# Two-layer retention and block-attention trunk on one core: weights loaded by halves of 0.5 MB with fewer bytes queued, embedding inputs loaded later, one normalisation moved to ScalarE, more buffers for turned tiles

## The chip, the cores and the metric

The kernel runs on one NeuronCore of a Trainium2 chip. The metric is the device time of one execution in microseconds (us). The kernel before was timed in three runs; their median is 311.43 us.

## What is computed

Two decoder layers over x of 256 tokens by 1024, all in float32:

```
for i in range(2):
    h = rms_norm(x, norm_g[i])
    rq, rk, rv, rz, mq, mk, mv, mz = split(h @ w_in[i], 8)        # 1024 x 4096, 512 columns each
    r = groupnorm(retention(rotary(rq), rotary(rk), rv)) * ret_norm_g[i] * silu(rz)     # 4 heads of 128
    m = moba(rms_norm(mq), rms_norm(mk), mv, rel_bias) * silu(mz)                       # 4 heads of 128
    x = x + concat(r, m) @ w_out[i]                               # 1024 x 1024
    gate = sigmoid(rms_norm(x) @ w_ple_gate[i])                   # 1024 x 1024
    x = x + gate * rms_norm(p[i] @ w_ple[i], ple_norm_g[i])       # p[i]: 256 x 256
```

With 256 tokens there is one block, so the block attention is causal softmax attention with a bias by distance. Retention is linear attention with a fixed decay; its per-head normalisation subtracts the mean of 128 outputs and divides by their deviation.

## The kernel before

**Products.** A float32 operand is split into a high part (rounded to the short form that TensorE multiplies) and the remainder. One product of 128 tokens, 128 inner elements and 512 columns is then three matmuls, `mm3` (L314 high times high, L315 high times low weights, L316 low times high weights). There are 408 such triples, 200 in layer 0 and 208 in layer 1, counted with the embedding's (L580 to L582); a set of weights serves both token halves m.

**Weights.** `Stage` (L245) stands for a 512 x 512 piece of a weight matrix, 1 MB. `gen` waits for one of four buffers `wst` of 1 MB and has SP issue the load (L261). `cast` then makes, for each half (two rows of 128), the high part on ScalarE (ACT, L271, tile wh) and the low part on VectorE (DVE, L273, tile wl); there are six pairs of wh and wl. A half serves 12 matmuls of 512 columns.

**Turned tiles.** Activations must be transposed before they are multiplied. ACT separates the 16-bit halves of a tile (`halves`, L450, tile u), SP issues a transposing DMA (`turned`, L460, tile w), and DVE copies the result into place (L469): into T for the heads of queries and keys, into PS for the probabilities, into tmp for the next product's operand, whose high part ACT makes (L486) and whose low part DVE makes (L488).

**The order** of all engines but TensorE's rows is chosen while the program is written, by a planner (`Flow`, L80). It keeps a clock per engine and a model of the DMA queue (`dma`), and lays each chain's next step when its engine, its buffers and its predecessors are free by its own clocks; among the ready steps the one with the lowest key goes first. Weight loads are held back while the modelled queue is more than `BACKLOG` ahead (L115). On the chip the resulting instruction streams are fixed: an engine, and SP's queue of DMA issues too, runs in that order and waits at an instruction whose semaphore isn't there yet.

**A layer** (`layer`, L606) runs: the projections MQ, MK, RQ, RK, MZ, MV, RV, RZ; between their matmuls, at points that the planner picks (`tick`), the attention scores (L751), attention output (L762), retention scores (L813) and retention output (L762 again); then the output projection, the embedding product (`embed`, L550) and the gate product, whose results update x (`gated`, L938). In layer 1 the MQ and MK projections are interleaved. `load_p` (L590) loads the embedding's inputs: pf (256 KB) and its gain gb, spread to all partitions (512 KB).

`ret_norm` (L819) takes statistics of the retention output on DVE, the inverse root on GpSimd (POOL, L502), and writes the normalised output on DVE (L838) into a tile T; `ret_gate` multiplies it by the gate (L855).

## Time and profile before

| | us |
|---|---|
| runs of the kernel | 310.88, 313.27, 311.43 (median 311.43) |
| the profiled execution | 310.27 |
| its span, first to last instruction | 308.5 |

The profiled execution is one run recorded by the hardware profiler; 1.8 us of it lie outside the span. All places in time below are us from the span's start. Matmul ends are modelled, so the pace of TensorE (PE) is read from the starts of successive matmuls: 0.227 us for 512 columns. A weight load (PEld) belongs to the matmul behind it.

### The profile page before, as it was taken

To read this page: it belongs to the slowest core of one execution; us is meant where nothing else is said; L and a number is where in the kernel's file an instruction comes from. 1 tells how busy PE (TensorE), PEld (TensorE's weight loads), DVE (VectorE), ACT (ScalarE), POOL (GpSimd) and SP (SyncE) were. 2 spreads that over 40 slices of the span, in tenths; PEclk is the share of its full clock that TensorE was granted. 3 is DMA by queue.
4 is the path that set the end of the run, shared out by engine and by line. 5 is a ranking of instruction groups with operands and counts; after the bars stand their busy time and mean duration, and the time that the engine had idled before them with its cause. 6 is when DMAs were issued, how large, how long until landed. Compare 5 with 4: busy or idle time off the path is not lost.

```text
span 308.5 us, 4105 instructions
## 1 busy us (share of the span) xinstructions
PE 300.1 (97%) x1393; PEld 247.6 (80%) x1393; DVE 254.4 (82%) x470; ACT 204.3 (66%) x342; POOL 32.8 (11%) x43
## 2 busy tenths in 40 slices
PE   8999999999999999999999999899999999999993
PEld 3888888878888888887878888688888888888783
DVE  3896898889887785799999595999988689739972
ACT  5879965995552566887588695499545438479611
POOL 5032100000002200031002220000000220001300
PEclk9999999999999999999999999999999999999999
DMA  7999999899963487583977889788897435784011
GB/s 257 413 425 407 270 321 287 230 295 305 324 184 139 147 227 259 90 300 136 295 212 188 293 269 227 191 215 235 282 363 203 166 136 132 259 155 69 1 70 69
DMA packets 54853, 69.76 MB, mean 226 GB/s; under 512 B 45484, under 2 KB 46256, under 8 KB 48688
## 3 DMA queue, kind: packets, MB, share of 16 engines
q1 hardware_dynamic: 54824, 69.50, 74.8%
q8 instruction: 11, 0.18, 0.3%
q14 instruction: 10, 0.08, 0.1%
q10 hardware_dynamic: 8, 0.00, 0.0%
HBM read 57.42 MB, written 1.05 MB: 190 GB/s over the span
## 4 chain that ended last, share of the span: by engine, by line
PE 69%; DVE 15%; DMA 11%; issue 2%; POOL 1%; ACT 1%; POOLq 0%; ACTq 0%; DVEq 0%
PE acc L315 21%; PE acc L316 21%; PE acc L314 21%; DMA w<-u 10%; DVE wl L273 5%; PE mix L762 3%; DVE tmp L469 2%; DVE E L569 1%; DVE a L488 1%; PE mix L813 1%; DMA a<-in_first 1%; DVE x_t L902 1%; DVE T L469 1%; PE mix L751 1%; DVE tok L668 1%
## 5 line engine op out<-in xcount | busy, mean ns | idle before, releaser
L315 PE MATMUL acc<-wl,a 128*128 128x512 f32 (+1 forms) x392 | 151.7, 387 | 0.7 <-DVE wl L273 0.5
L314 PE MATMUL acc<-wh,a 128*128 128x512 f32 (+1 forms) x392 | 152.2, 388 | 0.0
L316 PE MATMUL acc<-wh,a 128*128 128x512 f32 (+1 forms) x392 | 151.0, 385 | 0.3 <-DVE her L565 0.3
L273 DVE TENSOR_TENSOR wl<-wst,wh 128x1024 fp32r<-128x1024 f32 x96 | 114.8, 1219 | 8.5 <-ACT wh L271 8.4
L271 ACT CAST wh<-wst 128x1024 fp32r<-128x1024 f32 x96 | 98.6, 1052 | 25.3 <-PE acc L316 21.8
L315 PEld LDWEIGHTS acc<-wl,a 128*128 128x128 f32 x392 | 73.7, 188 | 17.7 <-DVE wl L273 2.1
L314 PEld LDWEIGHTS acc<-wh,a 128*128 128x128 f32 x392 | 73.8, 188 | 15.1 <-ACT wh L363 0.4
L316 PEld LDWEIGHTS acc<-wh,a 128*128 128x128 f32 x392 | 73.7, 188 | 15.2 <-DVE a L488 0.7
L450 ACT COPY u<-tok 128x1024 uint16<-128x1024 uint16 x30 | 31.5, 1049 | 19.7 <-DVE tok L668 7.4
L469 DVE COPY tmp<-w 128x512 uint16<-128x512 uint16 x40 | 16.5, 457 | 10.5 <-DMA w<-u 10.5
L486 ACT CAST a<-tmp 128x512 fp32r<-128x512 f32 x20 | 12.4, 622 | 18.3 <-DVE tmp L469 9.5
L502 POOL TENSOR_TENSOR ro<-rs_t,neghalf 128x4 f32<-128x4 f32 x4 | 7.7, 1914 | 132.7 <-DVE rs_t L500 132.7
L469 DVE COPY T<-w 128x512 uint16<-128x512 uint16 x32 | 12.8, 457 | 7.0 <-DMA w<-u 6.7
L450 ACT COPY u<-x_t 128x1024 uint16<-128x1024 uint16 x12 | 12.5, 1045 | 5.8 <-DVE x_t L902 3.4
L943 ACT ACTIVATE tmp<-acc,hr 128x512 f32<-128x512 f32 (+1 forms) x9 | 5.8, 640 | 12.8 <-PE acc L316 9.2
L488 DVE TENSOR_TENSOR a<-tmp,a 128x512 fp32r<-128x512 f32 x20 | 13.7, 684 | 0.0
L502 POOL TENSOR_TENSOR er<-rs_t,neghalf 128x1 f32<-128x1 f32 x4 | 4.9, 1230 | 67.3 <-DVE rs_t L500 63.2
L762 PEld LDWEIGHTS mix<-V,PS 128*128 128x128 f32 x96 | 11.3, 192 | 0.3
L644 POOL TENSOR_TENSOR qr<-qms,neghalf 128x4 f32<-128x4 f32 x8 | 8.4, 1063 | 28.7 <-DVE qms L642 15.9
L762 PE MATMUL mix<-V,PS 128*128 128x128 f32 x96 | 11.4, 275 | 0.0
L733 ACT ACTIVATE tok<-tok,nm 128x128 f32<-128x128 f32 (+1 forms) x16 | 7.1, 447 | 5.4 <-DVE nm L730 5.4
L946 DVE SCALAR_TENSOR_TENSOR tmp<-tmp,E 128x512 f32<-128x512 f32 (+1 forms) x9 | 5.6, 627 | 4.4 <-ACT tmp L943 4.4
(86 smaller groups left out, 241.1 us busy)
## 6 DMA issues: line engine op xcount, KB each, us to landing
wst<-in_w_in SPq DMA_DIRECT2D x30, 1024.0 KB, 5.6
wst<-in_w_out SPq DMA_DIRECT2D x8, 1024.0 KB, 5.8
wst<-in_w_gate SPq DMA_DIRECT2D x8, 1024.0 KB, 5.2
wst<-in_w_ple SPq DMA_DIRECT2D x2, 1024.0 KB, 5.0
wst<-in_rest SPq DMA_DIRECT2D x4, 384.0 KB, 7.0
a<-in_rest SPq DMA_DIRECT2D x3, 384.0 KB, 4.9
x_t<-in_x SPq DMA_DIRECT2D x2, 512.0 KB, 10.1
gb<-in_ple_g SPq DMA_DIRECT2D x2, 512.0 KB, 5.4
```

What stands on the lines that cost most here:

```text
L271: nc.scalar.copy(hi, s)
L273: nc.vector.tensor_tensor(lo, s, hi.bitcast(F32), op=ALU.subtract)
L314: nc.tensor.matmul(ps, ah, wh[:, kk, cols], start=start, stop=False)
L315: nc.tensor.matmul(ps, ah, wl[:, kk, cols], start=False, stop=False)
L316: nc.tensor.matmul(ps, al, wh[:, kk, cols], start=False, stop=stop)
L450: nc.scalar.copy(u, src.bitcast(U16).rearrange("p (n t) -> p t n", t=2))
L469: nc.vector.tensor_copy(v, w[:, t].rearrange("p (h b) k -> p h (b k)", h=v.shape[1]))
L486: nc.scalar.copy(h, src)
L488: nc.vector.tensor_tensor(a.lo[:, k0:k0 + 4, m * P:(m + 1) * P], src, h.bitcast(F32), op=ALU.subtract)
L502: nc.gpsimd.tensor_tensor(dst, t[:, :n], neghalf[:, :n], op=ALU.pow)
L644: nc.gpsimd.tensor_tensor(r, t, neghalf[:, :H], op=ALU.pow)
L762: nc.tensor.matmul(ps[:, h * DH:(h + 1) * DH], lhs(h, m, b), v[:, b, h * DH:(h + 1) * DH], start=b == 0, stop=b == m)
```

## The change

Weights are loaded by halves: 96 loads of 0.5 MB into eight buffers, instead of 48 of 1 MB into four (the same bytes in the same space). The planner's allowance for queued bytes is 9.0 us of its queue model early in the program, then 1.5, then 0.7 (before: none early, then 3.0). The embedding's inputs are loaded at the MV projection instead of right after MK. x is loaded in one DMA. The normalised retention output is written by ACT as scale times input plus bias, for which DVE makes a small tile mr. There are four u and three w buffers instead of three and two; the small statistics tiles have four buffers per name instead of eight. Keys (a higher number is less urgent) of two chains move: the embedding's normalisation from -5 to -2, the squares from 3 to 8. In the last layer the two outputs of the first 512 columns leave in one DMA. The matmuls are the same in number and kind; the planner sets the attention scores of each layer two triples earlier among them.

```diff
-BACKLOG = 3.0
-U_BUFS, W_BUFS, T_BUFS = 3, 2, 3
+U_BUFS, W_BUFS, T_BUFS = 4, 3, 3
...
-        return r if mb is None or self.dma < 30 else max(r, self.dma - BACKLOG)
+        return r if mb is None else max(r, self.dma - self.backlog())
+
+    def backlog(self):
+        return 9.0 if self.dma < 30 else 1.5 if self.dma < 60 else 0.7
...
-    wst_p = pool("wst", 4)
+    wst_p = pool("wst", 8)
...
-    sm = pool("sm", 8)
+    sm = pool("sm", 4)
...
-                flow.begin(self.gen(), lambda: due(2 * self.i) - 10, 0.0)
-
-        def gen(self):
-            yield ask(SP, 0.45, take=("wst",), mb=1.0)
-            self.st = wst_p.tile([P, 4, GW], F32, name="wst")
-            nc.sync.dma_start(self.st, self.src)
-            yield ask(SP, 0.0)
-            for c in range(2):
-                self.chains[c] = flow.begin(self.cast(c), lambda c=c: due(2 * self.i + c) - 7, flow.end)
-
-        def cast(self, c):
+                for c in range(2):
+                    self.chains[c] = flow.begin(self.gen(c), lambda c=c: due(2 * self.i + c) - 7, 0.0)
+
+        def gen(self, c):
+            yield ask(SP, 0.42, take=("wst",), mb=0.5)
+            s = wst_p.tile([P, 2, GW], F32, name="wst")
+            nc.sync.dma_start(s, self.src[:, 2 * c:2 * c + 2])
             yield ask(ACT, 0.955, take=("w",))
...
-    L_X = [flow.begin(load(lambda m=m: x_t[:, m], lambda m=m: x[:, m], 0.5), 10.0 + m, 0.0) for m in range(MT)]
+    L_X = flow.begin(load(lambda: x_t, lambda: x, 1.0), 10.0, 0.0)
...
-            ST_X[l, m, "E"] = flow.begin(scaled(m, ps), flow.soon(-5))
+            ST_X[l, m, "E"] = flow.begin(scaled(m, ps), flow.soon(-2))
...
+            mr = small(H, "mr")
+            yield ask(DVE, 0.15)
+            nc.vector.scalar_tensor_tensor(mr, mv[:, :, 0], -1.0, r2, op0=ALU.mult, op1=ALU.mult)
             for h in range(H):
                 sl = slice(h * DH, (h + 1) * DH)
-                yield ask(DVE, 0.32, take=() if m or h else ("T",))
+                yield ask(ACT, 0.19, take=() if m or h else ("T",))
...
-                nc.vector.tensor_scalar(o[:, sl], ps[:, sl], mv[:, h, 0:1], r2[:, h:h + 1],
-                                        op0=ALU.subtract, op1=ALU.mult)
+                nc.scalar.activation(o[:, sl], ps[:, sl], AF.Identity, bias=mr[:, h:h + 1], scale=r2[:, h:h + 1])
...
-        load_p(l)
         for g in ORDER[2:]:
+            if g == MV:
+                load_p(l)
             project((g,), by_m=g == RZ)
...
-            sq.append(flow.begin(squares([xs], SQ[m][:, n:n + 1]), flow.soon(3), flow.end))
+            sq.append(flow.begin(squares([xs], SQ[m][:, n:n + 1]), flow.soon(8), flow.end))
```

**SP's queue, layer 1, around the turned queries and keys of the attention.** w<-u is a turned tile; the last of the four before the scores is the second half of MK. Before:

```order
L241 DMA pf<-in_pT 128x512
L241 DMA gb<-in_ple_g 128x1024
L261 DMA wst<-in_w_in 128x2048
L460 DMA_TRANSPOSE w_1886<-u_1874 128x8x128
L261 DMA wst<-in_w_in 128x2048
L460 DMA_TRANSPOSE w_1914<-u_1900 128x8x128
```

After:

```order
L265 DMA wst<-in_w_in 128x1024
L455 DMA_TRANSPOSE w_1950<-u_1937 128x8x128
L265 DMA wst<-in_w_in 128x1024
L455 DMA_TRANSPOSE w_1982<-u_1958 128x8x128
L265 DMA wst<-in_w_in 128x1024 x4
```

One half of 0.5 MB stands ahead of each turned tile instead of a whole 1 MB (128x2048), and the loads of pf and gb are gone from here.

**DVE, layer 0, from the attention's third row of scores to the first low weights of MV.** L730 (after: L725) is the maximum of the scores, L663, L665 and L668 the rotary step of RK, L469 (after: L464) the copies of turned probabilities into PS. The last row of each piece begins with the low weights of MV's first half. Before:

```order
L730 TENSOR_REDUCE nm<-tok 128x2
L663 TENSOR_TENSOR tmp<-acc,cst 128x512
L665 TENSOR_TENSOR tok<-acc,cst 128x512
L668 TENSOR_TENSOR tok<-tok,tmp 128x512
L663 TENSOR_TENSOR tmp<-acc,cst 128x512
L273 TENSOR_TENSOR wl<-wst,wh 128x1024
L469 COPY PS<-w_646 128x4x128 x2
L665 TENSOR_TENSOR tok<-acc,cst 128x512
L469 COPY PS<-w_667 128x2x256 x2
L668 TENSOR_TENSOR tok<-tok,tmp 128x512
L273 TENSOR_TENSOR wl<-wst,wh 128x1024 x3
```

After:

```order
L725 TENSOR_REDUCE nm<-tok 128x2
L271 TENSOR_TENSOR wl<-wst,wh 128x1024 x2
L658 TENSOR_TENSOR tmp<-acc,cst 128x512
L660 TENSOR_TENSOR tok<-acc,cst 128x512
L464 COPY PS<-w_660 128x4x128 x2
L663 TENSOR_TENSOR tok<-tok,tmp 128x512
L464 COPY PS<-w_669 128x2x256 x2
L658 TENSOR_TENSOR tmp<-acc,cst 128x512
L660 TENSOR_TENSOR tok<-acc,cst 128x512
L663 TENSOR_TENSOR tok<-tok,tmp 128x512
L464 COPY PS<-w_697 128x2x256 x2
L271 TENSOR_TENSOR wl<-wst,wh 128x1024 x2
```

Two low weights stand between the maximum and MV's instead of one, and the third pair of copies into PS now comes ahead of MV's low weights.

**DVE, layer 0, end of the gate product and start of the update of x.** hr is a scale from GpSimd, L946 and L948 (after: L944 and L946) update x, L483 (after: L478) and L488 (after: L483) make the first operand of layer 1. Before:

```order
L926 TENSOR_SCALAR hr_1423<-r_1422 128x1
L946 SCALAR_TENSOR_TENSOR tmp<-tmp,E 128x512
L948 TENSOR_TENSOR x_t<-x_t,tmp 128x512
L273 TENSOR_TENSOR wl<-wst,wh 128x1024 x2
L946 SCALAR_TENSOR_TENSOR tmp<-tmp,E 128x512
L948 TENSOR_TENSOR x_t<-x_t,tmp 128x512
L273 TENSOR_TENSOR wl<-wst,wh 128x1024 x2
L469 COPY tmp<-w_1502 128x512 x2
L483 TENSOR_TENSOR tmp<-tmp,par 128x512
L946 SCALAR_TENSOR_TENSOR tmp<-tmp,E 128x512
L948 TENSOR_TENSOR x_t<-x_t,tmp 128x512
L488 TENSOR_TENSOR a<-tmp,a 128x4x128
```

After:

```order
L271 TENSOR_TENSOR wl<-wst,wh 128x1024
L924 TENSOR_SCALAR hr_1514<-r_1513 128x1
L944 SCALAR_TENSOR_TENSOR tmp<-tmp,E 128x512
L946 TENSOR_TENSOR x_t<-x_t,tmp 128x512
L271 TENSOR_TENSOR wl<-wst,wh 128x1024 x2
L944 SCALAR_TENSOR_TENSOR tmp<-tmp,E 128x512
L946 TENSOR_TENSOR x_t<-x_t,tmp 128x512
L271 TENSOR_TENSOR wl<-wst,wh 128x1024
L464 COPY tmp<-w_1571 128x512 x2
L478 TENSOR_TENSOR tmp<-tmp,par 128x512
L944 SCALAR_TENSOR_TENSOR tmp<-tmp,E 128x512
L946 TENSOR_TENSOR x_t<-x_t,tmp 128x512
```

One low weight has moved ahead of the first update of x; behind the last row shown here another low weight now comes before layer 1's first operand.

## Rows read from the trace of the kernel before

**Rows 1.** The page: span, busy time of each engine, and the span in 40 equal slices of 7.71 us, of which the busy tenths of the 16 DMA engines and what they moved.

```profile
span 308.5 us, 4105 instructions
PE 300.1 (97%) x1393; PEld 247.6 (80%) x1393; DVE 254.4 (82%) x470; ACT 204.3 (66%) x342; POOL 32.8 (11%) x43
...
DMA  7999999899963487583977889788897435784011
GB/s 257 413 425 407 270 321 287 230 295 305 324 184 139 147 227 259 90 300 136 295 212 188 293 269 227 191 215 235 282 363 203 166 136 132 259 155 69 1 70 69
```

**Rows 2.** Busy time of the engines in the stretch from 92 to 104 us (retention output) and from 125 to 148 us (end of layer 0): us, then PE, PEld, DVE, ACT, POOL with counts, PE's clock, DMA share, GB/s.

```profile
92.00:104.00 12.00, 12.00 (x67) 10.39 (x66) 9.36 (x32) 4.17 (x5) 3.83 (x2) 1.00 0.38 124
125.00:148.00 23.00, 22.94 (x101) 18.68 (x100) 22.27 (x43) 17.90 (x31) 4.23 (x4) 1.00 0.62 178
```

**Rows 3.** The chain that ended last: start, us, what. Two turned tiles of the gate product's operand, from issue to landing, and the piece right behind PE's last matmul.

```profile
120.88 4.15 DMA w<-u
...
269.69 5.27 DMA w<-u
...
303.88 0.48 ACT tmp L943
```

**Rows 4.** PE's instructions in order of time around its stalls: start, duration, line, operation, and in brackets idle time before.

```profile
63.00 0.39 PE L314 MATMUL acc<-wh,a 128*128 128x512 f32 x1
63.58 0.50 PE L315 MATMUL acc<-wl,a 128*128 128x512 f32 x1 [0.19 <-DVE wl L273]
...
144.96 0.39 PE L314 MATMUL acc<-wh,a 128*128 128x512 f32 x1
145.41 0.50 PE L315 MATMUL acc<-wl,a 128*128 128x512 f32 x1
...
153.94 0.39 PE L316 MATMUL acc<-wh,a 128*128 128x512 f32 x1
...
191.76 1.05 PE L751 MATMUL mix<-T 128*128 128x128 f32 x8
194.30 1.97 PE L751 MATMUL mix<-T 128*128 128x256 f32 x8 [1.49 <-DVE T L469]
...
288.75 0.40 PE L315 MATMUL acc<-wl,a 128*128 128x512 f32 x1
289.46 0.50 PE L316 MATMUL acc<-wh,a 128*128 128x512 f32 x1 [0.31 <-DVE her L565]
...
294.33 0.39 PE L316 MATMUL acc<-wh,a 128*128 128x512 f32 x1
294.56 0.39 PE L314 MATMUL acc<-wh,a 128*128 128x512 f32 x1
295.27 0.50 PE L315 MATMUL acc<-wl,a 128*128 128x512 f32 x1 [0.32 <-DVE wl L273]
```

**Rows 5.** DVE in order of time, at the places where a turned tile or a low weight is late.

```profile
54.83 0.80 DVE L469 COPY T<-w 128x512 uint16<-128x512 uint16 x2 [1.59 <-DMA w<-u]
55.52 0.67 DVE L730 TENSOR_REDUCE nm<-tok 128x2 f32<-128x512 f32 x1
56.11 0.68 DVE L663 TENSOR_TENSOR tmp<-acc,cst 128x512 f32<-128x512 f32 x1
...
62.30 2.36 DVE L273 TENSOR_TENSOR wl<-wst,wh 128x1024 fp32r<-128x1024 f32 x2
...
125.05 0.80 DVE L469 COPY tmp<-w 128x512 uint16<-128x512 uint16 x2 [3.68 <-DMA w<-u]
...
144.14 2.35 DVE L273 TENSOR_TENSOR wl<-wst,wh 128x1024 fp32r<-128x1024 f32 x2
...
152.77 0.69 DVE L488 TENSOR_TENSOR a<-tmp,a 128x512 fp32r<-128x512 f32 x1
...
193.36 0.79 DVE L469 COPY T<-w 128x512 uint16<-128x512 uint16 x2 [2.41 <-DMA w<-u]
...
274.99 0.80 DVE L469 COPY tmp<-w 128x512 uint16<-128x512 uint16 x2 [4.65 <-DMA w<-u]
```

**Rows 6.** The shortest, median and longest of the times to landing: first of the turned tiles (line L460), then of the 1 MB loads (L261).

```profile
DMA to landing us min/median/max: 3.0/3.9/11.4
...
DMA to landing us min/median/max: 4.7/5.4/12.0
```

**Rows 7.** SP's queue in order of time, layer 1 ahead of the attention scores: start, time that the issue took, line, DMA.

```profile
179.43 0.35 SPq L261 DMA_DIRECT2D wst<-in_w_in  x1
181.70 1.24 SPq L460 DMA_TRANSPOSE w<-u  x1
183.91 0.33 SPq L261 DMA_DIRECT2D wst<-in_w_in  x1
184.54 2.16 SPq L460 DMA_TRANSPOSE w<-u  x1
```

**Rows 8.** DMA issues: tile, queue, count, size of one, median us from issue to landing.

```profile
wst<-in_rest SPq DMA_DIRECT2D x4, 384.0 KB, 7.0
...
pf<-in_pT SPq DMA_DIRECT2D x2, 256.0 KB, 2.9
```

**Rows 9.** Groups of instructions by line and shape: busy us in total, mean ns of one, idle time before and what ended it.

```profile
L638 ACT ACTIVATE tmp<-acc 128x128 f32<-128x128 f32 x32 | 8.5, 287 | 1.0 <-PE acc L316 1.0
...
L838 DVE TENSOR_SCALAR T<-mix,bmv,ro 128x128 f32<-128x128 f32 x16 | 5.5, 405 | 0.1
```

More of the change, by code (lines that the diff above doesn't have):

```diff
@@ L114, in can @@
             r = max(r, min(self.free_at[s]))
-        return r if mb is None or self.dma < 30 else max(r, self.dma - BACKLOG)
+        return r if mb is None else max(r, self.dma - self.backlog())
+    def backlog(self):
+        return 9.0 if self.dma < 30 else 1.5 if self.dma < 60 else 0.7
     def pick(self):
-        best = None
         by = {}
@@ L123, in pick @@
                 by.setdefault(c.want[0], []).append((r, c))
+        best = None
         for eng, cs in by.items():
@@ L195, in pool @@
         return ctx.enter_context(tc.tile_pool(name=name, bufs=bufs, **kw))
-    flow = Flow(dict(wst=4, w=6, tmp=4, tok=3, u16=U_BUFS, w16=W_BUFS, T=T_BUFS, PS=1, V=1, G=1, acc=4, mix=4))
+    flow = Flow(dict(wst=8, w=6, tmp=4, tok=3, u16=U_BUFS, w16=W_BUFS, T=T_BUFS, PS=1, V=1, G=1, acc=4, mix=4))
     cp = pool("cp", 1)
-    wst_p = pool("wst", 4)
+    wst_p = pool("wst", 8)
     wh_p = pool("wh", 6)
@@ L269, in cast @@
             lo = wl_p.tile([P, 2, GW], F32R, name="wl")
-            s = self.st[:, 2 * c:2 * c + 2]
             nc.scalar.copy(hi, s)
@@ L274, in cast @@
             self.parts[c] = hi, lo
-            if c:
-                flow.free("wst")
+            flow.free("wst")
         def part(self, c):
             now[0] = max(now[0], 2 * self.i + c)
-            while self.chains[c] is None:
-                flow.force()
             flow.need(self.chains[c])
@@ L374, in first_block @@
         nc.vector.tensor_tensor(lo, w, hi.bitcast(F32), op=ALU.subtract)
-        if k in (5, 7):
+        if k >= 4:
             flow.free("wst")
@@ L391, in first_blocks @@
         for k in range(KT):
-            if k in (4, 6):
+            if k >= 4:
                 flow.take("wst")
-                home, at = wst_p.tile([P, 4, GW], F32, name="wst").rearrange("p k n -> p (k n)"), 0
+                home, at = wst_p.tile([P, 2, GW], F32, name="wst").rearrange("p k n -> p (k n)"), 0
             c = flow.begin(first_block(k, home, at), k - 20.0, 0.0)
@@ L461, in turned @@
                           transpose=True)
-        yield ask(DVE, 0.35, take=take)
-        flow.free("u16")
-        dst = raw()
+        dst = None
         for t in range(2):
-            if t:
-                yield ask(DVE, 0.35)
+            yield ask(DVE, 0.35, take=() if t else take)
+            if not t:
+                flow.free("u16")
+                dst = raw()
             v = dst[:, t]
@@ L518, in tile_hybrid_trunk @@
     E, ST_X = {}, {}
-    DONE = [[Mark() for _ in range(2)] for _ in range(MT)]
+    DONE = [[[Mark() for _ in range(2)] for _ in range(MT)] for _ in range(DEPTH)]
     def x_stats(l, m, after=()):
@@ L871, in layer @@
         for m in range(MT):
-            ST_X[l, m, 0] = flow.begin(x_stats(l, m, DONE[m] if l else (L_X[m],)), flow.soon(3 if l else 12))
+            ST_X[l, m, 0] = flow.begin(x_stats(l, m, DONE[l - 1][m] if l else (L_X,)), flow.soon(3 if l else 12))
         if l == 0:
@@ L949, in gated @@
             flow.free("tmp")
-            flow.reach(DONE[m][n])
-            if last:
+            flow.reach(DONE[l][m][n])
+            if last and n:
                 yield ask(SP, 0.35, mb=width / 2048)
                 nc.sync.dma_start(out[m * P:(m + 1) * P, sl], x_t[:, m, sl])
+            elif last and m:
+                yield ask(SP, 0.35, after=(DONE[l][0][0],), mb=0.5)
+                nc.sync.dma_start(out[:, sl].rearrange("(m p) n -> p m n", m=MT), x_t[:, :, sl])
+            elif last:
+                return
             else:
```

## Prediction

> **What bounds the kernel now.** I read the page first. PE is busy for 300.1 of 308.5 us, DVE for 82%, ACT for 66% [rows 1], and PE's granted clock is at full speed in the stretches looked at [rows 2], which is 2.4 GHz. The change leaves the matmuls as they are, so it can win only where PE stands still: before its first product, behind its last (at 303.9 us, after which 4.6 us of gate, update and store follow [rows 3]), and in between. The head and the tail have the same instructions on the path in both programs, so I give them nothing. Next I read PE's instructions in order of time: the idle time in their brackets is little, nearly all of it waiting for DVE, but modelled matmul ends hide part of a stall, so I took the starts [rows 4]. Two successive 512-column matmuls start 0.23 us apart (294.33, 294.56). Where they don't, the excess is the loss:
> at 63, 63.58 - 63.00 - 0.23 = 0.35, plus some 0.11 at the next matmul, together 0.46 (low weights late);
> at 145, 0.22 + 0.11 = 0.33 (low weights late);
> at 192, 194.30 - 191.76 = 2.54 for eight narrow matmuls whose ordinary spacing of 0.11 would make 0.9: 1.65 (turned keys late);
> at 289, 0.48 + 0.11 = 0.59 (low part of an operand late);
> at 295, the same 0.59 (low weights late).
> These five sum to 3.6 us, or 1.2% of the run. That is the most that the change can win; my forecast is how much of it goes, less what comes in its place. (Within 1%, 3.1 us, is about what a measurement of this kernel can't tell from no change.)
>
> What is behind them: DVE copies a turned tile as soon as it lands, in a fixed order, and waits for it with everything behind. It waits 2.41 us at 193.36, 1.59 at 54.83, 3.68 at 125.05 and 4.65 at 274.99 [rows 5]; after the last two it is all but full (22.27 of 23 us [rows 2]). A turned tile lands 3.0 us after its issue at best, but up to 11.4 [rows 6]: the loads issued ahead of it on the same queue land first.
>
> **The change part by part.**
>
> *Layer 1's scores.* The last turned key tile is issued at 184.54, right behind a 1 MB load at 183.91, with another from 179.43 before it [rows 7], and its copy starts at 193.36 [rows 5]: 8.8 us. Now a half stands ahead of it, another ahead of the tile before, and pf and gb (768 KB) are gone. The queue moved 227 to 269 GB/s in these slices [rows 1], so 0.52 MB take about 2 us. The tile lands between 184.5 + 3.0 and 184.5 + 3.0 + 2.0, at 187.5 to 189.5, and two copies of 0.40 us make the keys ready by 190.3. PE wants them after its first eight narrow matmuls, at 191.76 + 0.9 = 192.7 today; the planner sets the scores two triples earlier (6 x 0.227 = 1.4 us) and earlier stalls may shrink by 0.7, so at 190.6. The 1.65 us go. Bounds: all of it, or nothing (a tile that lands as late as now makes PE wait just until the same moment). I take -1.65.
>
> *End of layer 1.* No load is left behind the last w_gate here. That one is now 0.5 MB and lands earlier: a 1 MB load takes 4.7 us at least, 256 KB 2.9 [rows 8, 6], so a half some 3.5. The first turned tile of the gate's operand then lands near 3.0 us after its issue at 269.69 instead of 5.27 [rows 3]: DVE starts its full stretch 1 to 2 us before 274.99 [rows 5]. The late low weights at 295.27 have the same DVE work ahead of them as before, so they come 1 to 2 us earlier; PE's want is 0.48 us. The operand at 289.46 also has one low weight (1.2 us) fewer ahead of it. Both stalls go: -1.18, bounds -1.18 and 0. I take -1.0.
>
> *End of layer 0.* The same tile lands 4.15 us after its issue at 120.88 today [rows 3]; with the half, about 1 us earlier. The low weights of 144.14 have moved ahead of one update of x (two instructions of 0.68), so they are ready 2 us earlier and the 0.33 goes. But layer 1's first low operand (L488, 152.77 + 0.69 = 153.46) gets one low weight more ahead of it, + 1.2 - 1.0 = 153.66, and PE wants it at 153.94 - 0.33 = 153.6 [rows 4, 5]. Between 0 and 1.2 (if the earlier start fails) is lost there; I take 0.3, near the end that the earlier start gives. Net 0, bounds -0.33 and +0.9.
>
> *Layer 0, low weights of MV.* In SP's queue 9.5 MB of weights stand ahead of the second turned tile of RQ, before it was 10 MB with pf and gb: 1.25 MB less. The DMA engines are at 9 tenths from 8 to 54 us [rows 1], so at 287 to 425 GB/s the tile lands 3.1 to 4.6 us before 54.83, at about 51 (its own 3.0 us allow 49.7). Behind it DVE now has, up to the end of MV's low weights: copies 0.7, a row of scores 0.6 and its maximum 0.6, two low weights 2.3, two rotary steps 3.7, three pairs of copies 2.1, the low weights 1.1, by the starts in [rows 5] (0.6 from L730 to L663, 1.13 for a low weight): 11.1, so 62.1. PE wants them at 63.2. Waiting for the turned probabilities can cost up to 1 us of that. If the tile landed at 54.83 as before, they would be ready at 65.9, 2.7 late. So the stall is 0 to 2.7, against 0.46 before; I take 0.2, near the first end, since 51 follows from the bytes: -0.26.
>
> *Retention's normalised output.* 16 instructions of 405 ns leave DVE and 16 come to ACT, each between 0.25 us (L638, 287 ns with some overlap) and 0.4; four small ones are added to DVE [rows 9]. It saves DVE about 2.2 us per layer in a stretch where it is busy 9.36 of 12 us and ACT 4.17 [rows 2]; PE waits for nothing there. Worth 0 on the path. If ACT's casts came late by 4 x 0.3, the weights still have several us in hand.
>
> *The rest at 0.* 48 more issues of 0.33 us on SP [rows 7], which is off the path; x in one DMA, whose bytes are the same; the joined output store, early enough to land before the last stores; fewer small buffers, whose readers are long done. Cover gone, each would show as a late turned tile at 1 us or less.
>
> *Weights by halves, the rule against it.* The DMA engines moved 413 GB/s in the slice from 7.7 us on, with the 384 KB pieces of the first product on the queue [rows 1, 8]. The Trainium skill (DMA: Bandwidth & Descriptors, Measured) asks to batch DMAs to at least 1 MiB for 75% of peak, and gives 2.0 us fixed plus bytes over 436 GB/s for one on another issue path; by that a half alone is an estimated 3.2 us. The trace agrees only where a load stands alone on the queue; queued behind each other they overlap.
>
> Sum: -1.65 - 1.0 + 0 - 0.26 = -2.9. Every engine's order is new, and DVE is full in four stretches, so I add one new stall of the size of the present small ones (0.33 to 0.59): +0.5. That gives -2.4: 310.27 - 2.4 = 307.9 for an execution like the profiled one. The median of the three runs is 1.16 above that one, so 311.43 - 2.4 = 309.0.
>
> **The rivals.**
> *All stalls go.* Nothing new comes: -3.6, 307.8; the earlier turned tiles help everywhere, as above. Against it: the 0.3 and 0.2 left are narrow.
> *The gain is eaten.* The scores' stall goes, but DVE's full stretches give it back: MV 0.46 to 1.5, layer 1's first operand 0.9, the end of layer 1 unchanged: -1.65 + 1.0 + 0.9 - 0.33 = about 0, 311.3. For it: the tight places of the new order; against: every wait of DVE there begins with a late turned tile.
> *Slower: the queue is as full as before, and the new order waits for it.* Then the turned tiles land as late as now, the change doesn't do what it says, and DVE's order, which counts on them early, stops the low weights: +2.2 in layer 0 (2.7 - 0.46), about 2 at the same place of layer 1, +0.9 at layer 1's first operand, nothing won at the scores: +5.1, 316.5. It decides if the RQ tile lands less than 2 us earlier. Against it: 1.25 MB fewer ahead.
> *Slower: loads one at a time.* A half alone takes about 3.5 us (between 2.9 and 4.7 [rows 8, 6]), PE uses it in 12 x 0.227 = 2.7; over some 88 halves that is +70, 380. It needs one load in flight; the order shows up to six in a row. The batching rule of the Trainium skill, above, would have it so.
>
> **How the numbers follow.** My forecast (gain 1.0 to 3.1) 0.54, all stalls go 0.21, eaten 0.19, full queue 0.05, one at a time 0.01. Faster by over 1% is the second case and a little of the first: 0.23; slower is the last two: 0.06; the same 0.71. The range reaches from the full gain with 0.4 for the runs' spread, 307.4, to the eaten case, 311.3.
>
> **What would show it.** Right: copies of turned keys at about 189 in layer 1 and no wait of PE at the second scores; DVE's stretch at the end of layer 1 starting by 273.5; the RQ tile in layer 0 copied by 52; PE's starts without gaps at 289 and 295; ACT writing T in about 0.3 us each. Wrong: turned tiles landing after 5 us or more at these places, casts on ACT waiting for DMA in the middle of a layer, or new gaps in PE's starts over 1 us at MV or at layer 1's first rows.

## The result and the profile after

The changed kernel takes 308.88 us (median of 19 runs, 307.55 to 310.74) where the kernel before takes 311.28 (19 runs): ratio 0.9926, interval 0.9904 to 0.9948. Timed again, beside other runs of the kernel before, it took 310.01 (12 runs) against 311.30 (29 runs): 0.9970, interval 0.9935 to 1.0005. So the gain is some 0.3 to 0.7%, clear of zero in the first timing and not quite in the second, and inside the forecast's band (308.88 for a predicted 309.0). The profiled executions show less: 309.39 with a span of 307.5, and 310.28 with a span of 308.5 the second time, against 310.27 with 308.5 before. The profiled execution of before happened to lie 1.0 under its own median, and those of after 0.5 and 0.3 above theirs. What the typical run of before loses beyond its profile is not shown by any trace here. Ratios leave out runs more than 1.5% above the fastest of the same kernel and those at half clock, which matters for the first timing of halves and limit together (experiment 4): its 0.9946 rests on 6 of its 12 runs, while the 11 at full clock, taken together, have a median of 311.85 against 311.17, a ratio of 1.002.

The head of the page after, to be laid beside [rows 1]: PE is as busy as before, so the page shows nothing of what changed.

```profile
span 307.5 us, 4248 instructions
...
PE 299.6 (97%) x1393; PEld 248.2 (81%) x1393; DVE 250.9 (82%) x458; ACT 210.6 (68%) x358; POOL 32.6 (11%) x43
```

So I read PE's starts again. The rows after that answer to [rows 4]: start, duration, line, operation, and in brackets the idle time before.

```profile
64.19 0.39 PE L309 MATMUL acc<-wh,a 128*128 128x512 f32 x1
66.27 0.50 PE L310 MATMUL acc<-wl,a 128*128 128x512 f32 x1 [1.69 <-DVE wl L271]
...
192.51 2.78 PE L746 MATMUL mix<-T 128*128 128x128 f32 x16
...
294.29 0.39 PE L309 MATMUL acc<-wh,a 128*128 128x512 f32 x1
294.88 0.50 PE L310 MATMUL acc<-wl,a 128*128 128x512 f32 x1 [0.20 <-DVE wl L271]
```

The 16 score matmuls of layer 1 now run through, and the stops at 145 and 289 are gone. In their place stands one of 64.19 to 66.27, and a short one stays at 294. The second profile of the same program stops once more, at the end of layer 0, and longer at 294:

```profile
154.82 0.39 PE L310 MATMUL acc<-wl,a 128*128 128x512 f32 x1
156.19 0.50 PE L311 MATMUL acc<-wh,a 128*128 128x512 f32 x1 [0.98 <-DVE a L483]
...
294.41 0.39 PE L309 MATMUL acc<-wh,a 128*128 128x512 f32 x1
295.77 0.50 PE L310 MATMUL acc<-wl,a 128*128 128x512 f32 x1 [0.98 <-DVE wl L271]
```

Summed by place, over all matmuls: what successive starts are apart beyond the usual spacing of their shape, in us, for every profiled execution at full clock (tail: from PE's last end to the end of the span). In the last row MV stands for 59 to 77 us, and some 3.2 of its 9.72 are matmuls at half clock behind two stops. Outside these places only four lose over 0.1 (halves alone 1.3 around 96, old limit 1.2 at 216, limit alone 0.4 at 48, seven tiles on ACT's queue 0.3 in layer 1).

| kernel | head, to 16 us | MV, 62 to 72 | end of layer 0, 138 to 166 | scores, layer 1 | end of layer 1, from 275 | tail | span | ratio to before, interval |
|---|---|---|---|---|---|---|---|---|
| before | 1.21 | 0.48 | 0.50 | 1.76 | 1.26 | 4.64 | 308.5 | 1 |
| after | 2.49 | 1.99 | 0.00 | 0.01 | 0.49 | 4.10 | 307.5 | 0.9926 (0.9904 to 0.9948) |
| after, again | 1.24 | 1.73 | 1.62 | 0.01 | 1.31 | 4.10 | 308.5 | 0.9970 (0.9935 to 1.0005) |
| before + halves | 1.31 | 3.11 | 2.54 | 4.25 | 2.93 | 4.52 | 318.6 | 1.0313 (1.0272 to 1.0355) |
| before + limit | 1.44 | 0.75 | 5.26 | 0.01 | 0.00 | 4.62 | 310.9 | 1.0011 (0.9980 to 1.0042) |
| before + both | 1.13 | 2.75 | 0.86 | 0.00 | 1.69 | 4.24 | 309.3 | 0.9946 (0.9908 to 0.9983), again 0.9996 (0.9966 to 1.0026) |
| after, old limit | 1.21 | 1.40 | 2.91 | 1.91 | 0.23 | 4.07 | 311.8 | 1.0093 (1.0059 to 1.0127) |
| after, pf and gb early | 1.54 | 1.59 | 1.23 | 0.01 | 0.75 | 4.08 | 307.7 | 0.9925 (0.9896 to 0.9955) |
| after, old buffers | 2.68 | 1.27 | 0.64 | 0.01 | 2.03 | 4.09 | 309.2 | 0.9972 (0.9940 to 1.0004) |
| after, norm on DVE | 1.07 | 1.59 | 1.04 | 0.01 | 2.29 | 4.08 | 308.6 | 0.9988 (0.9963 to 1.0012) |
| the same, again | 1.38 | 2.07 | 2.08 | 0.00 | 2.38 | 4.08 | 310.7 | 1.0020 (0.9996 to 1.0043) |
| after, probabilities due later | 1.05 | 1.28 | 1.24 | 0.00 | 0.61 | 4.08 | 306.9 | 0.9960 (0.9933 to 0.9986) |
| after, 7 tiles on ACT's queue | 2.86 | 9.72 | 0.00 | 0.82 | 0.69 | 4.07 | 316.9 | 1.0306 (1.0262 to 1.0350) |

The head's losses, 1.1 to 2.9, are not all the program's: one program lost 2.49 and 1.24 there, and the first product's loads landed after 6.7 us (median) in the profile of after and after 5.6 in its second.

DVE after, at the places of [rows 5]; the start of the last full stretch stands in the last two rows.

```profile
54.27 0.82 DVE L464 COPY T<-w 128x512 uint16<-128x512 uint16 x2 [1.57 <-DMA w<-u]
...
64.32 0.79 DVE L464 COPY PS<-w 128x512 uint16<-128x512 uint16 x2 [0.37 <-DMA w<-u]
65.00 2.35 DVE L271 TENSOR_TENSOR wl<-wst,wh 128x1024 fp32r<-128x1024 f32 x2
...
190.54 0.79 DVE L464 COPY T<-w 128x512 uint16<-128x512 uint16 x2
...
273.93 0.80 DVE L464 COPY tmp<-w 128x512 uint16<-128x512 uint16 x2 [3.23 <-DMA w<-u]
...
293.60 2.36 DVE L271 TENSOR_TENSOR wl<-wst,wh 128x1024 fp32r<-128x1024 f32 x2
```

SP's queue ahead of layer 1's scores, against [rows 7], then the shortest, median and longest time to landing of the turned tiles, against [rows 6]: one half stands ahead of a turned tile, and the longest falls from 11.4 to 7.8.

```profile
183.28 1.24 SPq L455 DMA_TRANSPOSE w<-u  x1
184.61 0.53 SPq L265 DMA_DIRECT2D wst<-in_w_in  x1
185.49 1.24 SPq L455 DMA_TRANSPOSE w<-u  x1
...
DMA to landing us min/median/max: 3.0/3.7/7.8
```

ACT's new instructions (against [rows 9]) take 6.0 us in 16, 0.38 of its time each:

```profile
L836 ACT ACTIVATE T<-mix,mr,ro 128x128 f32<-128x128 f32 x16 | 6.0, 462 | 4.0 <-DVE mr L829 4.0
```

### The profile page after: what moved, and what is told of

Same layout as the page of the kernel before. It is cut to its first block, busy times and chain, and to the rows that moved or that the text cites. A ratio compares the mean times of both kernels' runs of the same rounds, so it can differ in the third digit from the quotient of the medians.

```text
span 307.5 us, 4248 instructions
## 1 busy us (share of the span) xinstructions
PE 299.6 (97%) x1393; PEld 248.2 (81%) x1393; DVE 250.9 (82%) x458; ACT 210.6 (68%) x358; POOL 32.6 (11%) x43
## 3 DMA queue, kind: packets, MB, share of 16 engines
HBM read 57.42 MB, written 1.05 MB: 190 GB/s over the span
## 4 chain that ended last, share of the span: by engine, by line
PE 77%; DMA 8%; DVE 7%; issue 3%; ACT 2%; POOL 1%; POOLq 0%; SPq 0%; ACTq 0%; DVEq 0%
PE acc L310 23%; PE acc L311 23%; PE acc L309 23%; DMA w<-u 5%; PE mix L757 3%; DVE wl L271 3%; DMA a<-in_rest 2%; DMA wst<-in_w_gate 2%; PE mix L808 1%; POOL er L497 1%; PE mix L746 1%; ACT wh L269 1%; DVE a L483 1%; DVE tmp L464 1%; PE mix L576 1%
## 5 line engine op out<-in xcount | busy, mean ns | idle before, releaser
L464 DVE COPY tmp<-w 128x512 uint16<-128x512 uint16 x40 | 16.2, 456 | 8.7 <-DMA w<-u 8.7
L497 POOL TENSOR_TENSOR ro<-rs_t,neghalf 128x4 f32<-128x4 f32 x4 | 4.9, 1234 | 127.2 <-DVE rs_t L495 127.2
L464 DVE COPY T<-w 128x512 uint16<-128x512 uint16 x32 | 12.8, 455 | 3.5 <-DMA w<-u 3.5
L483 DVE TENSOR_TENSOR a<-tmp,a 128x512 fp32r<-128x512 f32 x20 | 13.7, 686 | 0.8 <-ACT a L481 0.8
L639 POOL TENSOR_TENSOR qr<-qms,neghalf 128x4 f32<-128x4 f32 x8 | 11.5, 1445 | 13.0 <-DVE qms L637 13.0
L757 PE MATMUL mix<-V,PS 128*128 128x128 f32 x96 | 11.4, 275 | 0.0
L633 ACT ACTIVATE tmp<-acc 128x128 f32<-128x128 f32 x32 | 8.5, 287 | 1.6 <-PE acc L311 1.6
```

The costliest lines, as they stand in the source:

```text
L464: nc.vector.tensor_copy(v, w[:, t].rearrange("p (h b) k -> p h (b k)", h=v.shape[1]))
L483: nc.vector.tensor_tensor(a.lo[:, k0:k0 + 4, m * P:(m + 1) * P], src, h.bitcast(F32), op=ALU.subtract)
L497: nc.gpsimd.tensor_tensor(dst, t[:, :n], neghalf[:, :n], op=ALU.pow)
L639: nc.gpsimd.tensor_tensor(r, t, neghalf[:, :H], op=ALU.pow)
L757: nc.tensor.matmul(ps[:, h * DH:(h + 1) * DH], lhs(h, m, b), v[:, b, h * DH:(h + 1) * DH], start=b == 0, stop=b == m)
```

## The experiments

**1. Halves alone, in the kernel before.**

```diff
-                flow.begin(self.gen(), lambda: due(2 * self.i) - 10, 0.0)
+                for c in range(2):
+                    self.chains[c] = flow.begin(self.gen(c), lambda c=c: due(2 * self.i + c) - 7, 0.0)
...
+            nc.sync.dma_start(s, self.src[:, 2 * c:2 * c + 2])
```

> The kernel before with the weight loads cut into halves of 0.5 MB, each its own chain with its own staging buffer, and nothing else of the change. SP's order puts pf, gb (768 KB) and two or three halves between the second turned query tile and the last turned key tile of layer 1, 1.75 to 2.25 MB, where the kernel before has 2.77 MB. Theory (the gain is turned tiles that land earlier because fewer bytes stand ahead of them): the last turned key tile lands about 1 to 2 us earlier, PE's stall at layer 1's scores falls from 1.65 us to 0.7 or less, the time from 311.3 to about 310.3 (ratio 0.995 to 0.998). Rival 1 (the gain needs the smaller backlog or the later pf and gb): the stall stays over 1.2 us and the time within 0.2% of before. Rival 2 (DVE's relief by the norm on ACT, or the buffers, is what paid): the same, no gain from halves.

Measured: 320.75 us, ratio 1.0313. All three expectations failed, since none had a slowdown; halving by itself costs 10 us. DVE waits 28.8 us for turned tiles (17.3 for tmp, 10.0 for T, 1.5 for PS) where before waits 17.9 and after 13.0 (15.2 in its second profile). At layer 1's scores PE stands still longer than before; the row, and two 3 us later that start 0.43 us apart instead of 0.227:

```profile
199.87 2.65 PE L743 MATMUL mix<-T 128*128 128x256 f32 x8 [2.34 <-DVE T L461]
...
203.17 0.63 PE L308 MATMUL acc<-wh,a 128*128 128x512 f32 x1
203.60 0.63 PE L306 MATMUL acc<-wh,a 128*128 128x512 f32 x1
```

**2. The limit alone, in the kernel before.**

```diff
-        return r if mb is None or self.dma < 30 else max(r, self.dma - BACKLOG)
+        return r if mb is None else max(r, self.dma - (9.0 if self.dma < 30 else 1.5 if self.dma < 60 else 0.7))
```

> The kernel before with only the planner's limit on outstanding bytes changed (9, then 1.5, then 0.7 us of transfers instead of none, then 3.0); loads of 1 MB, the old buffers, norm on VectorE. In SP's order gb now stands behind a turned key tile of layer 1, pf and two or three 1 MB loads stay among the turned tiles: about 2.3 to 3.3 MB. Theory (bytes ahead of the turned tiles): little is won at the scores, the stall stays between 1.0 and 1.65 us, and the time within 0.3% of before. Rival (a small backlog alone is what paid): the stall goes and the time is 309.5 or less (ratio 0.994).

Measured: 311.49 us, ratio 1.0011. Time as the theory said, place as the rival said: the scores' stop is gone, and 5.26 us are lost at the end of layer 0 (1.5 of them at half clock behind the stop). This run does not show that the keys land early enough by themselves: PE comes to the scores 6.9 us later than before (198.62 for 191.76; two triples more stand ahead of them, and more was lost earlier), and the last keys are copied only 2.1 later (195.44 for 193.36).

At the stop of layer 0 a turned tile is issued 0.4 us behind a load of 1 MB and lands after 5.9 us, at 154.0. But DVE does not wait for it: in the planner's new order an update of x and a low weight stand ahead of the copy, and DVE comes to it at 154.29. So the next operand is late by what stands ahead of it on DVE and not by this landing, and PE waits. SP's row, the tile's landing, DVE's rows, then PE's:

```profile
148.13 1.24 SPq L460 DMA_TRANSPOSE w<-u  x1
...
DMA to landing us min/median/max: 5.9/5.9/5.9
...
153.15 1.22 DVE L273 TENSOR_TENSOR wl<-wst,wh 128x1024 fp32r<-128x1024 f32 x1
154.29 0.79 DVE L469 COPY tmp<-w 128x512 uint16<-128x512 uint16 x2
...
154.21 0.39 PE L316 MATMUL acc<-wh,a 128*128 128x512 f32 x1
156.78 0.50 PE L314 MATMUL acc<-wh,a 128*128 128x512 f32 x1 [2.19 <-ACT a L486]
```

**3. The old limit, in the kernel after.**

```diff
-        return r if mb is None else max(r, self.dma - self.backlog())
+        return r if mb is None or self.dma < 30 else max(r, self.dma - 3.0)
```

> The kernel after with the old limit on outstanding transfers (none in the first 30 us, then 3.0 us) and everything else of the change. In layer 1 SP's order around the turned keys differs from the kernel after by one half (two instead of one ahead of the last). Theory (bytes ahead of the turned tiles): scores in layer 1 stall 0 to 0.5 us, so the time is within 0.3% of the kernel after there; in layer 0 the low weights of MV are placed as before or later than the third tile of probabilities, stall 0.5 to 2 us. Time about 309 to 309.6 (ratio 0.993 to 0.995). Rival (the small backlog is what paid): the stall of 1.65 at layer 1's scores comes back, about 310.5 or more (ratio 0.998).

Measured: 313.67 us, ratio 1.0093. The rival was right: the scores stop again for 1.91 us. Two halves now stand between the last two turned keys, and the last lands after 6.7 us instead of the 4.4 of the kernel after (SP's rows and the landing):

```profile
185.73 1.24 SPq L455 DMA_TRANSPOSE w<-u  x1
187.06 1.73 SPq L265 DMA_DIRECT2D wst<-in_w_in  x2
188.89 1.24 SPq L455 DMA_TRANSPOSE w<-u  x1
...
DMA to landing us min/median/max: 6.7/6.7/6.7
```

The longer landing is 2.3 us of the delay. Another 3.4 come from the issue, at 188.89 instead of 185.49: ACT makes this tile's u only at 187.50, behind two casts, and in the kernel after at 184.41. PE comes to the scores 1.4 later here. So the limit acts by the order of ACT too, and not by the queue alone.

**4. Halves and limit together, in the kernel before** (both diffs of 1 and 2), and once more.

> The kernel before with the two parts together that cost 10 us (halves alone) and 1 us (the small limit on outstanding transfers alone): weight halves and the small limit, but the old place of pf and gb, the norm on VectorE, the old buffers and key stages. Theory now (halves and the small limit pay only together, by what stands ahead of the turned tiles): between the second turned query and the last turned key of layer 1 stand pf and two halves (1.25 to 1.3 MB; before 2.77 MB), so the stall at layer 1's scores is under 0.5 us and the time 308.5 to 309.8 (ratio 0.993 to 0.997), that is most of the gain of the whole change. Rival 1 (the later pf and gb, the buffers or the norm are needed): over 310.5, with a stall over 1 us at the scores or at the low weights of MV. Rival 2 (each edit only reshuffles the planner's order, and the times are chance): anything, with stalls at places that no queue explains.

> Before with halves and the small limit together, once more, for a profile at full clock (the first was taken at 0.56). Theory: no stall over 0.5 us at layer 1's scores, where before lost 1.65; 0.5 to 1.5 us at the low weights of MV; ratio to before 0.992 to 0.998, between 0 and 0.4% above the kernel after. Rival (the remaining parts of the change, norm and buffers and the later pf and gb, carry half of the gain or more): 0.4% or more above the kernel after.

Measured: 0.9946, and on the second chip 311.20 us, 0.9996, where the kernel after ran at 310.01. The scores do not stop, as the theory had it. The low weights of MV do, for 2.75 us, more than the 0.5 to 1.5 expected. So the two parts turn a loss of 3.1% into no change; a gain of their own is not shown (the 0.9946 holds for half of its runs only). On the second chip the rest of the change carries 0.26%, which these intervals do not separate from zero.

Taken together, the scores' stop is there in the three profiled kernels that have the old limit (1.76, 4.25, 1.91) and, but for the seven tiles on ACT's queue, under 0.02 in each that has the new one. The kernel after with the old limit differs from the kernel after in nothing else, so there the limit is what removed it. Halves without it cost time (1.0313, and 1.0093 in the kernel after). Whether the limit needs the halves is not shown: its ratio is 1.0011 with loads of 1 MB, and 0.9946 and 0.9996 with halves. Nor were the bytes in the queue and the order varied apart, since the planner orders every engine anew for each limit.

**5. The embedding's inputs early again, in the kernel after.**

```diff
             project((MQ, MK))
+        load_p(l)
         for g in ORDER[2:]:
-            if g == MV:
-                load_p(l)
```

> The kernel after with pf and gb (768 KB per layer) loaded right behind the projection of MK, as before. Theory: the small limit spreads them among the turned tiles (SP's order in layer 1 is half, turned tile, pf, half, two turned tiles, gb), so at most 0.25 MB more stand ahead of the last turned key: it lands at most 1 us later, a stall of 0 to 0.4 us at layer 1's scores, and the time is within 0.5 us of the kernel after (ratio to before 0.992 to 0.996). Rival (pf and gb out of the way is a main part of the gain): a stall over 0.8 us at the scores and 310 or more.

Measured: 309.39 us, 0.9925. As the theory said: no stop at the scores; pf and gb are worth nothing that can be measured once the limit spreads them.

**6. The old buffers, in the kernel after.**

```diff
-U_BUFS, W_BUFS, T_BUFS = 4, 3, 3
+U_BUFS, W_BUFS, T_BUFS = 3, 2, 3
```

> The kernel after with the old 3 and 2 buffers for the tiles ahead of and behind the turning transfer. SP's order in layer 1 is that of the kernel after; in layer 0 the order has the first low weight of MV ahead of the third probability tile. Theory: the buffers matter little: no stall over 0.4 us at layer 1's scores, 0.6 to 1.4 us at the low weights of MV, time 308.3 to 309.3 (ratio 0.991 to 0.996). Rival (a turning transfer waits for a free buffer): turned tiles are issued 1 us or more later than in the kernel after, stalls over 0.8 us in layer 1, 310 or more.

Measured: 310.27 us, 0.9972. Inconclusive: the scores and MV (1.27) are as the theory said, but 2.03 us are lost at the end of layer 1, where the order is that of the kernel after, and the interval overlaps both theories. The rival's late issue does not show there: retention's second turned tile is issued at 258.64, in the two profiles of the kernel after at 258.47 and 258.59. It lands after 6.3 us instead of 5.6 and 5.8.

**7. Retention's norm on DVE, in the kernel after,** and once more beside the kernel after on one chip.

```diff
-                nc.scalar.activation(o[:, sl], ps[:, sl], AF.Identity, bias=mr[:, h:h + 1], scale=r2[:, h:h + 1])
+                nc.vector.tensor_scalar(o[:, sl], ps[:, sl], mv[:, h, 0:1], r2[:, h:h + 1],
+                                        op0=ALU.subtract, op1=ALU.mult)
```

> The kernel after with retention's normalised output on VectorE again (8 instructions of 405 ns per layer instead of 8 on ScalarE). SP's order is that of the kernel after. Theory: the 2 us of VectorE's time per layer stand in a stretch where PE waits for nothing: the time is within 0.4 us of the kernel after (ratio 0.991 to 0.995), stalls at the same places as there, about 1.9 us at MV and under 0.6 near 294. Rival (VectorE is the limit and its relief is the gain): stalls of 0.8 to 2 us behind the norm (between 75 and 100 us, and 210 to 235 us), 310 or more.

> The kernel after with retention's normalised output on VectorE, once more, on the same chip as the kernel after. Its first 12 runs were 2 us above those of the kernel after, while PE lost nothing in the stretches of the norm (75 to 100 and 210 to 235 us), but 2 us near 292 to 295, where the order of VectorE and SP is that of the kernel after. Theory (the norm itself costs nothing; the 2 us are chance or chip): within 0.3% of the kernel after on this chip, the loss near 294 under 1.2 us. Rival (VectorE's relief is worth 2 us): 0.4 to 0.8% above the kernel after again, the loss near 292 to 295 again over 1.5 us.

> The kernel after once more, unchanged, beside the same runs of before as the three below. Theory: what its first profile shows at the head (2.3 us lost before 10 us, where before lost 1.2) and at 294 us (0.5 us) hangs on when DMAs land and moves by about 1 us from one execution to the next, while the 1.9 us at the low weights of MV near 64 us, where VectorE's order waits for a turned tile, stay within 0.6 of that; ratio to before 0.990 to 0.996. Rival (all of it is fixed by the order): the same losses at the same places within 0.3 us, the head's too.

Measured: norm on DVE 311.33 (0.9988), then 311.83 (1.0020) beside 310.01 (0.9970) for the kernel after. Twice 0.5 to 0.6% above it (the intervals of the second pair just overlap), and both times with 2.3 to 2.4 us lost at the end of layer 1 and nothing near the norm: the theory fell, the rival of the second text was right in time and place. The way from the norm to that place, by DVE's rows; first the kernel after (its second profile): the gates, the second turned tile of retention's output, the first update of x.

```profile
255.35 0.69 DVE L682 SCALAR_TENSOR_TENSOR G<-tmp,acc 128x512 f32<-128x512 f32 x1 [0.55 <-ACT tmp L678]
...
264.43 0.80 DVE L464 COPY tmp<-w 128x512 uint16<-128x512 uint16 x2 [2.22 <-DMA w<-u]
...
268.75 0.68 DVE L900 TENSOR_TENSOR x_t<-acc,x_t 128x512 f32<-128x512 f32 x1
...
274.83 0.47 DVE L464 COPY tmp<-w 128x512 uint16<-128x512 uint16 x1 [4.01 <-DMA w<-u]
```

Then the norm on DVE, its second profile, in which PE runs 1.13 us later in this stretch:

```profile
253.11 1.37 DVE L833 TENSOR_SCALAR T<-mix,bmv,ro 128x128 f32<-128x128 f32 x4
...
257.50 0.69 DVE L682 SCALAR_TENSOR_TENSOR G<-tmp,acc 128x512 f32<-128x512 f32 x1 [0.57 <-ACT tmp L678]
...
266.45 0.80 DVE L464 COPY tmp<-w 128x512 uint16<-128x512 uint16 x2 [2.10 <-DMA w<-u]
...
270.77 1.28 DVE L898 TENSOR_TENSOR x_t<-acc,x_t 128x512 f32<-128x512 f32 x2
...
277.10 0.46 DVE L464 COPY tmp<-w 128x512 uint16<-128x512 uint16 x1 [5.05 <-DMA w<-u]
```

Beyond PE's 1.13 the gate is 1.02 later, the turned tile 0.89, the update of x 0.89, and the first copy of DVE's last stretch 1.14. That stretch takes the same 22.0 us in every kernel with this order: from that copy to the end of the last two low weights (after: 273.93 to 293.60 + 2.36 = 295.96, its second profile 274.83 to 296.85, norm on DVE 275.00 to 297.03 and 277.10 to 299.11), and PE ends 7.5 us behind it in all four. So from the gate of retention on, the run's end hangs on DVE and on the landings of the turned tiles between, not on how early PE is there. The first profile of norm on DVE says the same: PE is 0.85 earlier in this stretch than in the kernel after's second profile, the gate 0.18 later and the first copy 0.17 later.

Across the experiments the gain shows only with the norm on ACT: without it the kernel after stands at 0.9988 and 1.0020, and halves with limit, which have it on DVE too, at 0.9996 on the second chip.

The second profile of after also answers its own text: the head moved by 1.25 us between two executions, the end of layer 1 by 0.8, and MV by 0.26. Its end of layer 0 (1.62 against 0.00) was not foreseen.

**8. The probabilities' chains due later, in the kernel after,** so that DVE makes the first low weight of MV ahead of the third probability tile.

```diff
-                PC[m, h0] = flow.begin(probs(m, h0, per, ps), flow.soon(3))
+                PC[m, h0] = flow.begin(probs(m, h0, per, ps), flow.soon(5))
```

> The kernel after with the chain of a probability tile due 5 us instead of 3 after its scores. VectorE's order then has the first low weight of MV ahead of the copies of the third probability tile in layer 0; layer 1 is planned as in the kernel after. Theory (the 1.96 us that PE loses at about 64 us come from that copy, which waits for the tile to land with the low weights queued behind it): the loss falls to between 0 and 0.8 us, and the time to about 307.4 (ratio to before 0.986 to 0.990). Rival 1 (the low weights are late because the load or the cast is late, or VectorE is full): the loss stays over 1.4 us and the time at 308.9. Rival 2 (the wait only moves: the second product waits for the probabilities, or a later turned tile is late): the loss at 64 goes, a new one over 0.8 us shows within the next 25 us.

Measured: 309.44 us, 0.9960. MV falls from 1.99 and 1.73 to 1.28, not to 0.8 or less. The order was part of it: with it the old buffers have 1.27, and the five profiles with the order and limit of the kernel after have 1.59 to 2.07. The other part is a full DVE (the low weight starts at 62.96, right behind DVE's preceding instruction). The 1.24 at the end of layer 0 are like those of the kernel after's second profile. No better than the kernel after.

**9. Seven of the turned tiles issued by ACT, in the kernel after;** the planned order stays.

```diff
+    NTH, ON_ACT = [0], (5, 6, 9, 26, 27, 39, 40)
...
-        nc.sync.dma_start(w.rearrange("p t h k -> p (t h) k"), u.rearrange("p t n -> p (t n)"),
+        NTH[0] += 1
+        (nc.scalar if NTH[0] in ON_ACT else nc.sync).dma_start(w.rearrange("p t h k -> p (t h) k"), u.rearrange("p t n -> p (t n)"),
```

> The kernel after in the same order, but seven of the 42 turning transfers (both of RQ and the third of the probabilities in layer 0, both of MK in layer 1, the first two of the gate's operand at the end of layer 1) are issued by ScalarE on its own DMA queue instead of SP's. Theory (a turned tile lands late because it stands behind loads in SP's queue): these seven land 3.0 to 3.4 us after their issue (in the kernel after RQ's took 4.4 and 5.4, the third of the probabilities 4.9, MK's last 4.4, the gate's first 3.8); each costs ScalarE some 1.2 us of issue; the loss at 64 us falls by 0.5 to 1.2, that near 294 goes, the time falls by 0 to 1 us against the kernel after. Rival (what the tile waits for is the DMA engines, which all queues share): latencies as before, 4 us and more, and the time the same or up to 1 us longer by ScalarE's issues.

Measured: 319.99 us, ratio 1.0306, worse than either text. The seven landed after 4.1 to 10.6 us, RQ's two after 7.9 and 10.6 (after, on SP's queue: 4.4 and 5.5, in its second profile 5.7 and 5.2). ACT's issues, the landings of the seven, and PE at the low weights that DVE could make only behind RQ's second tile:

```profile
47.79 1.32 ACTq L458 DMA_TRANSPOSE w<-u  x1
...
49.23 3.16 ACTq L458 DMA_TRANSPOSE w<-u  x1
...
DMA to landing us min/median/max: 4.1/6.9/10.6
...
59.12 0.39 PE L309 MATMUL acc<-wh,a 128*128 128x512 f32 x1
63.17 0.53 PE L310 MATMUL acc<-wl,a 128*128 128x512 f32 x1 [3.67 <-DVE wl L271]
```

So a queue of its own does not take a turned tile past the loads. (In SP's queue a turned tile also holds back the loads behind it: those that SP issued at 48.8 and 50.0 here came at 50.8 and later in the kernel after. How much of the delay is theirs was not tried.)

## Why the prediction came out right

The time is right, and in good part by luck. One of its steps stands in size, the scores. The low weights of MV, the ends of both layers and the added stall were mis-sized, and by the profiles the terms sum to -0.9 and 0.1 where the working has -2.4.

*Layer 1's scores, -1.65.* Measured -1.75 in both profiles. The keys' last copies start at 190.54, 1 us later than the working had the tile land, and still ahead of the scores. But I credited the half in place of 1 MB and the absent pf and gb. Experiment 3 shows that it is the planner's limit, and experiment 5 that with it pf and gb do nothing.

*Low weights of MV, -0.26.* Measured +1.5 and +1.25, inside the bounds (0 to 2.7 lost). The step that failed is "the tile lands at about 51": RQ's second tile is copied at 54.27. It landed after 5.5 us instead of 8.1, which is the gain that the working counted on, but it was issued 2.1 us later than in the kernel before. Of these, 0.7 are DVE's rotary steps, which end at 46.25 instead of 45.56; the rest is ACT, which makes both of RQ's u tiles behind a cast that waits for PE (SP's row before, then SP's and ACT's after):

```profile
46.71 2.26 SPq L460 DMA_TRANSPOSE w<-u  x1
...
48.80 1.98 SPq L455 DMA_TRANSPOSE w<-u  x1
...
45.45 1.05 ACT L269 CAST wh<-wst 128x1024 fp32r<-128x1024 f32 x1 [2.36 <-PE acc L311]
46.40 1.99 ACT L445 COPY u<-tok 128x1024 uint16<-128x1024 uint16 x2
```

Behind the copy 11.9 us of DVE's work follow, for the 11.1 of the working, with 0.37 of waiting for the third probabilities.

*End of layer 0, net 0.* Measured -0.5 and +1.1: the bounds of -0.33 and +0.9 held neither. The step that failed is the tile that lands "about 1 us earlier": it was issued at 122.67 and 121.60 instead of 120.88, and its copies start at 126.16 and 125.86, behind the 125.05 of [rows 5]. The low part of layer 1's operand is then ready at 155.92 and 156.14, not at 153.66 (DVE's rows in the two profiles):

```profile
155.24 0.68 DVE L483 TENSOR_TENSOR a<-tmp,a 128x512 fp32r<-128x512 f32 x1
...
155.45 0.69 DVE L483 TENSOR_TENSOR a<-tmp,a 128x512 fp32r<-128x512 f32 x1
```

In the first profile PE comes there at 156.25, late by what it lost at the head, and does not wait. In the second it would be there 1.2 us earlier and waits. So DVE sets the time at this place, and what PE has lost ahead of it is not lost again: head, MV and end of layer 0 together lose 4.48 and 4.59 in the two profiles.

*End of layer 1, -1.0.* Measured -0.8 and +0.05. The step that failed is the landing near 3.0 us after an issue at 269.69: the tile was issued at 270.16 and 270.54 and landed after 3.7 and 4.3 us. The stretch starts 1.06 and 0.16 us earlier than the 274.99 of [rows 5], but takes 22.0 us where before's took 21.4 (274.99 to 296.35). The wait at 289 went and the one at 294 stayed. The start by 273.5 that I named was missed by 0.4 and 1.3.

*Retention's norm, 0.* Against the kernel before this can't be read alone; in the new order it is worth 0.5% (experiment 7). "PE waits for nothing there" was true and not the question: the stretch feeds the chain that ends the run.

*The rest at 0.* The tail is 0.54 shorter (4.64 to 4.10). All kernels with the joined output store have 4.07 to 4.10, all without it 4.24 to 4.64; that the store is the cause was not tried by itself. *One new stall, +0.5:* the new ones are the terms above.

By these terms the first profile gives -1.75 + 1.5 - 0.5 - 0.8 - 0.5 + 1.3 (head) - 0.1 (elsewhere) = -0.9, the second -1.75 + 1.25 + 1.1 + 0.05 - 0.5 = 0.1. The medians say -2.4 and -1.3. The differences of 1.4 to 1.5 are left open: with one profile of before, its own spread at the head and at the layers' ends isn't known. So the forecast of 307.9 for a profiled execution was missed by 1.5 and 2.4 (309.39 and 310.28), and that the medians of the first timing lie 2.4 apart, as forecast, is luck as far as the traces tell.

Of the rivals, the eaten gain came nearest in mechanism and the forecast in time: in the second profile all four terms of that rival are there (scores -1.75, MV +1.25, end of layer 0 +1.1, end of layer 1 unchanged). The batching rule that I weighed against the change (the Trainium skill, DMA: Bandwidth & Descriptors, Measured) would have halves slower; halves alone did cost 3.1%, but with the limit they cost nothing (0.9996 on the second chip), so bytes per DMA are not what decided.

## What to carry to other kernels

Where two engines are both nearly full, look at the end of each stage for the stretch that starts with one landing and has a fixed length; what moves that landing moves the end of the run, however far off the path its engine looks. Try finer transfers together with a smaller number outstanding: halves alone lost 3.1% here, the limit alone won nothing, and together they lost nothing. And two profiles of one program tell which of its small waits are fixed by the program: those at the head and at the layers' ends, which moved by 0.8 to 1.6 us, were not.

## What the runs showed of the hardware

A turning transfer on a second queue was slower beside loads than in the loads' queue (7.9 and 10.6 us against 4.4 and 5.5, or 5.7 and 5.2 in the second profile). The Trainium skill (DMA: Bandwidth & Descriptors, Queues, rings and completion order) states that each DMA engine takes turns between queues packet by packet; by that a tile on its own queue should not have to wait out the loads' backlog. The trace of experiment 9 agrees with the turns, and not with what I took from them. Its packets by queue (q1 is SP's, q10 ACT's; packets, MB, share of 16 engines' time), from 47.8 to 51.4 us and from 53.4 to 55.5:

```profile
q1 hardware_dynamic: 359, 1.34, 103.6%
...
q1 hardware_dynamic: 139, 0.52, 67.2%
q10 hardware_dynamic: 133, 0.03, 8.3%
```

From 53.4 on the two queues move about as many packets each, but by these rows a packet of the loads holds some 3.7 KB and one of the turned tile 0.2, so the loads take nearly all of the bytes. And for the 3.6 us before 51.4, with the first tile issued at 47.79, no packet of ACT's queue moved at all; why is open.

TensorE's granted clock fell from 2.4 to 1.2 GHz behind some stops and not behind others. With seven tiles on ACT's queue, after the stop that ended at 63.17, the stretch (columns: stretch, its length, then busy time of PE, PEld, DVE, ACT, POOL, PE's clock, DMA share, GB/s):

```profile
63.00:67.00 4.00, 3.83 (x10) 3.01 (x11) 4.00 (x9) 3.27 (x6) 0.00 (x0) 0.57 0.79 187
```

Matmuls then started 0.43 us apart instead of 0.227, which cost another 1.6 us for eight. The same followed stops of 2.42 us (same run, clock 0.59 from 73 to 77 us), 2.35 (experiment 2, 0.68 from 157 to 162) and 2.51 (experiment 1, 0.57 from 201 to 205), but not the 2.63 at MV in halves with limit, where the clock stayed at 1.00. So the length of a stop alone does not tell.
